# Products of 512 columns issued as two of 256, and their moving operands placed on multiples of 64 bytes

## The chip, the cores and the metric

One core of a Trainium2 chip runs the kernel. The metric is the device time of one execution in microseconds. TensorE multiplies: a product has a stationary operand (`lhsT`, 128 x 128), for which a weight load is recorded ahead of it, and a moving operand (`rhs`), whose columns stream through. VectorE (DVE) and ScalarE (ACT) take results out of PSUM and prepare operands, GpSimd (POOL) does little, and SyncE (SP) issues most of the DMAs.

## The reference

One decoder layer on a sequence of 512 positions with 1024 channels, in float32:

```python
h = rmsnorm(x, ln1_g)
z = h @ w_in                                   # 1024 x 8968
# columns of z: A sliding-window attention, B convolution module, C forgetting attention,
#               D block attention, and 4 x 1024 gate logits
gates = sigmoid(gz + b_gate)
proj  = einsum('bsnc,ncd->bsnd', branches, w_br)   # 4 branches, 512 -> 1024 each
x = x + (gates * proj).sum(branch) @ w_out         # 1024 x 1024
u = causal_depthwise_conv(rmsnorm(x, ln2_g) @ w_up, ffn_conv_w, ffn_conv_b)   # 1024 x 5632, width 3
x = x + (silu(g_ff) * v_ff) @ w_down               # 2816 x 1024
out = rmsnorm(x, final_g)
```

## The kernel before

Float32 products are made of three: every operand is split into a rounded part and a rest (`hi`, `lo`, type float32r), and a product is hi x hi, lo x hi and hi x lo, all added up in one PSUM bank of 512 columns. So nearly all of TensorE's work consists of chains of products `PE.matmul(ps, lhsT=..., rhs=..., start=..., stop=...)`, the first of which (`start`) writes the bank and the others add to it.

The work is a list of *units* (line 254 on). A unit of `t_mm` (line 232, the product on line 243) makes 128 output channels for all 512 positions: a chain of 3 x 8 products (3 x 4 for the branch projections), with the split weights `whi`/`wlo` stationary and the 512 positions of the activations moving. The activations are `hh`/`hl` (the normed input; `hh2`/`hl2`, which the trace also calls hh and hl, for the FFN) or the branch outputs `y`. There are 106 units with hh/hl (62 of the input projection and gates, 44 of the up projection) and 32 with y. `v_units` (line 278, product on line 294) are the other way round: positions stationary, 256 or 264 weight columns moving. `wo_half0` (line 957) and `wo_half1` (line 999) are the two halves of the output projection, with the merged branches stationary and 512 columns of weights moving, the second half's held in `WO` (`woh`, `wol`). `wd_mm` (line 1115) is the down projection: `ah`/`al` stationary, 512 weight columns moving, in the streamed `whi`/`wlo` or in `wdh`/`wdl`, the weights of the last 8 blocks of the second half, which are kept in the tags of `hh` and `hl` (line 1202). In the second half the last 128 positions are worked in two banks of 256 columns each (line 1126), so these products have 256 columns already.

In between the units, *pieces* of the attention heads are put in by a fixed table of steps (`STAGES`, `head_pieces`): scores (lines 451, 452, 565, 566), transposes of the probabilities (479, 596), and the product with the values (`pv`, lines 500 and 619). `pv` of a full head adds to one bank eight products of 512, 384, 256 and 128 columns, two of each, with the same `v` stationary in both of a pair. The order within each engine is the order in which the program writes the instructions (`manual_schedule`); the loop at line 1393 interleaves units, pieces, evictions, weight splits (lines 179, 180) and the steps of the width-31 convolution.

Weights come through a ring of `raw` tiles (2) filled by SP, and are split by ACT (hi) and DVE (lo) into rings `whi` and `wlo` of 3 tiles each.

The pools stand in SBUF like stacks. P0, on the left, holds in this order `ident` (512 bytes of each partition), `hh` and `hl` (16,384 each), `pcA`, `pcB`, `pcC` (368, 496, 512), `nsk`, `sk`, `bfg` (32 each), and then the rings raw, whi and wlo, which are allocated later. Behind it come the pools of the stages: PI, then P1 (attention), then PX (`x1`, `ss2`) and PW (`woh`, `wol`). On the right stands PY, with `acc` and the ring of y tiles (merged branches too), and after it PF (`ah`, `al`).

Of the kernel before, what the change touches and what calls it, by code (L numbers as in the profile page):

```python
# [8 lines left out]
F32 = mybir.dt.float32  # L9
# [9 lines left out]
KD = D // 128  # L19
NT = S // 128  # L20
# [33 lines left out]
def hybrid_layer_kernel(ctx: ExitStack, tc: tile.TileContext, x, ln1_g, w_in, b_gate, b_fgate, sinks,  # L54
# [3 lines left out]
    PE, ACT, DVE, SP = nc.tensor, nc.scalar, nc.vector, nc.sync  # L58
# [16 lines left out]
    P0 = pool("p0")  # L75
    PD = pool("pd", space=PSUM)
    PDR = pool("pdr", space=DRAM)
# [11 lines left out]
    nsk = P0.tile([128, 8], F32, name="nsk")  # L89
    sk = P0.tile([128, 8], F32, name="sk")  # L90
    bfg = P0.tile([128, 8], F32, name="bfg")

    def col_gate(n, j):
        return pcA[:, n * 8 + j:n * 8 + j + 1]
# [129 lines left out]
        return [Half(raw, slice(k, k + 4), slice(0, n)) for k in (0, 4)]  # L224


    class Unit:
        def __init__(self, hs, mm, ev, adv=True):
            self.hs, self.mm, self.ev, self.adv = hs, mm, ev, adv
# [2 lines left out]
    def t_mm(hf, c0, mh, ml, nk):  # L232

        def go(mid=None, at_k=0):
            ps = dense_ps()
            h = hf[0]
            n = 0
            for k in range(nk):
                if mid and k == at_k:
                    mid()  # L240
                wh, wl = h.hi[:, k, c0:c0 + 128], h.lo[:, k, c0:c0 + 128]
                for a, b in ((wh, mh(k)), (wl, mh(k)), (wh, ml(k))):
                    PE.matmul(ps, lhsT=a, rhs=b, start=n == 0, stop=n == 3 * nk - 1)  # L243
                    n += 1
            return ps
        return go
# [16 lines left out]
        return u  # L263


    PY = pool("py", side="right")
    acc = PY.tile([128, KD, S], F32, name="acc")

# [169 lines left out]
    def full_head(br, h):  # L438
        key = (br, h)
        o = live[key] = {}  # L440

        def qk(blocks):
            sk_ = stack[key]
            b2 = sk_["A"] if br == BR_D else sk_["G"]
            nr = 68
            ps = ctxP["s"]()
            c = 0
            for qb in blocks:
                n = (qb + 1) * 128
                qs = slice(qb * 128, qb * 128 + 128)  # L450
                PE.matmul(ps[:, c:c + n], lhsT=sk_["A"][:, qs], rhs=sk_["D"][:, :n], start=True, stop=False)  # L451
                PE.matmul(ps[:, c:c + n], lhsT=b2[:nr, qs], rhs=sk_["E"][:nr, :n], start=False, stop=True)  # L452
                o["s", qb] = ps[:, c:c + n]
                c += n

        def sm(blocks):
            P1 = ctxP["p1"]
            if "P" not in o:
                o["P"] = P1.tile([128, 1280], F32, name="P", tag="P", bufs=2)
                o["nm"] = P1.tile([128, 4], F32, name="nm", tag="nm", bufs=2)  # L460
                o["sm"] = P1.tile([128, 4], F32, name="sm", tag="sm", bufs=2)
                o["rc"] = P1.tile([128, 4], F32, name="rc", tag="rc", bufs=2)
            bias = ctxP["mask"] if br == BR_C else stack[key]["B"]
            for qb in blocks:
                n = (qb + 1) * 128
                soft(o["P"], slice(PO[qb], PO[qb] + n), o["s", qb], n, bias[:, 512 - n:], o["nm"], o["sm"], qb, BIG)

        def norm():
            DVE.reciprocal(o["rc"], o["sm"])
            for qb in range(NT):  # L470
                sl = slice(PO[qb], PO[qb] + (qb + 1) * 128)
                DVE.tensor_scalar(o["P"][:, sl], o["P"][:, sl], o["rc"][:, qb:qb + 1], None, op0=OP.mult)  # L472

        def tr(kbs):
            ps = ctxP["t"]()
            c = 0
            for kb in kbs:
                for qb in range(kb, NT):
                    PE.transpose(ps[:, c:c + 128], o["P"][:, PO[qb] + kb * 128:PO[qb] + kb * 128 + 128], ident)  # L479
                    c += 128  # L480
            o["t", kbs] = ps, c

        TO = {0: 0, 1: 512, 3: 896, 2: 1024}

        def tev(kbs):
            P1 = ctxP["p1"]
            if "PT" not in o:
                o["PT"] = (P1.tile([128, 1280], R32, name="PTh", tag="PTh", bufs=1),
                           P1.tile([128, 1280], R32, name="PTl", tag="PTl", bufs=1))
            ps, c = o["t", kbs]  # L490
            sl = slice(TO[kbs[0]], TO[kbs[0]] + c)
            ACT.activation(o["PT"][0][:, sl], ps[:, :c], AF.Copy)  # L492

        def tlo(kbs):
            ph, pl = o["PT"]
            ps, c = o["t", kbs]
            sl = slice(TO[kbs[0]], TO[kbs[0]] + c)
            DVE.tensor_tensor(pl[:, sl], ps[:, :c], f(ph[:, sl]), op=OP.subtract)

        def pv():  # L500
            ps = ctxP["y"]()
            v = Vt[br, h // 4]
            for kb in range(NT):
                n = (NT - kb) * 128
                for i, pt in enumerate(o["PT"]):
                    PE.matmul(ps[:, kb * 128:], lhsT=v[:, kb, h % 4, :], rhs=pt[:, TO[kb]:TO[kb] + n],  # L506
                              start=kb == 0 and i == 0, stop=kb == NT - 1 and i == 1, skip_group_check=True)
            o["y"] = ps

        def pvev():  # L510
            y_add(br, h, o["y"])

        def pvhl():
            y_out(br, h)
            del live[key]

        return [
            [(lambda: qk((0, 1)), lambda: sm((0, 1)))],
            [(lambda: qk((2,)), lambda: sm((2,)))],
            [(lambda: qk((3,)), lambda: sm((3,)), norm)],  # L520
            [(lambda: tr((0,)), lambda: tev((0,)), lambda: tlo((0,)))],
            [(lambda: tr((1, 3)), lambda: tev((1, 3)), lambda: tlo((1, 3)))],
            [(lambda: tr((2,)), lambda: tev((2,)), lambda: tlo((2,)))],
            [(pv, pvev, pvhl)],
        ]
# [416 lines left out]
    def wo_load():  # L942
        PX = ctxP["px"] = pool("px")
        for t in range(NT):
            xt = PX.tile([128, D], F32, name="x1_%d" % t)
            SP.dma_start(xt, dap(x, t * 128 * D, [[D, 128], [1, D]]))
            x1.append(xt)
        PW = ctxP["pw"] = pool("pw")
        WO["h"] = PW.tile([128, KD, 512], R32, name="woh")
        WO["l"] = PW.tile([128, KD, 512], R32, name="wol")  # L950
        n2["g"] = PW.tile([128, D], F32, name="g2")
        SP.dma_start(n2["g"], dap(ln2_g, 0, [[0, 128], [1, D]]))
        n2["ss"] = PX.tile([128, 2, NT], F32, name="ss2")

    oa = []

    def wo_half0(j0, hs):
        def mm():
            if j0 == 0:
                oa.extend(w_ps() for _ in range(NT))  # L960
            for k in (j0, j0 + 1):
                wh, wl = hs[0].hi[:, k - j0, :], hs[0].lo[:, k - j0, :]
                m = merged[k]
                for t in range(NT):
                    a, b = m[:, 0, t * 128:t * 128 + 128], m[:, 1, t * 128:t * 128 + 128]
                    for i, (l, r) in enumerate(((a, wh), (a, wl), (b, wh))):
                        PE.matmul(oa[t], lhsT=l, rhs=r, start=k == 0 and i == 0, stop=k == KD - 1 and i == 2)  # L967

        def ev(_):
            if j0 == 6:  # L970
                for t in range(NT):
                    wo_ev(t, 0, oa[t])
        add(hs, mm, ev)
# [25 lines left out]
    def wo_half1(t):  # L999
        def mm():  # L1000
            if t == 0:
                n2["hh"] = P0.tile([128, KD, S], R32, name="hh2", tag="hh")
                n2["hl"] = P0.tile([128, KD, S], R32, name="hl2", tag="hl")
            ps = dense_ps()
            for k in range(KD):
                m = merged[k]
                a, b = m[:, 0, t * 128:t * 128 + 128], m[:, 1, t * 128:t * 128 + 128]
                for i, (l, r) in enumerate(((a, WO["h"]), (a, WO["l"]), (b, WO["h"]))):
                    PE.matmul(ps, lhsT=l, rhs=r[:, k, :], start=k == 0 and i == 0, stop=k == KD - 1 and i == 2)  # L1009
            return ps  # L1010

        def ev(ps):
            wo_ev(t, 1, ps)
        u = add([], mm, ev)
        return u
# [99 lines left out]
    def wd_mm(ps, k, t, wh, wl, first_k, last_k):  # L1115
        a, b = ffn["ah"][:, k, t * 128:t * 128 + 128], ffn["al"][:, k, t * 128:t * 128 + 128]
        for i, (l, r) in enumerate(((a, wh), (a, wl), (b, wh))):
            PE.matmul(ps, lhsT=l, rhs=r, start=k == first_k and i == 0, stop=k == last_k and i == 2)  # L1118

    def wd_unit(k0, half, hs):  # L1120
        def mm():
# [84 lines left out]
    for half, end in ((0, NF), (1, KRES)):  # L1206
        for k0 in range(0, end, 4):
            nk = min(4, end - k0)
# [245 lines left out]
    ctxP["pf"].release()  # L1454
    ctxP["px"].release()
    ctxP["w"].release()
    for p in (PDR, PD, P0):
        p.release()


# [40 lines left out]
```

## Time and profile before

| | |
|---|---|
| median of 3 runs | 1014.49 us (1014.19 to 1014.76) |
| profiled execution | 1014.47 us, span 1012.7 us |
| instructions | 12462, of them 4840 products and 4840 weight loads |
| PE busy | 1001.2 us (99%) |
| PEld busy | 824.6 us (81%) |
| DVE busy | 667.0 us (66%) |
| ACT busy | 448.3 us (44%) |
| DMA | 102.18 MB, mean 101 GB/s |

The span runs from the first to the last instruction of the execution. PE's busy time is the union of its products, each from its start to its modelled end; since products overlap, it is no measure of how well the engine is used. The time that a product takes from the next one is the distance between their starts.

### The profile page before, as it was taken

How to read it: one execution, taken by the hardware profiler on the slowest of the kernel's cores; microseconds unless marked ns; L12 is line 12 of the kernel's file. 1: busy time of each engine (PE TensorE's matmuls, PEld its weight loads, DVE VectorE, ACT ScalarE, POOL GpSimd, SP SyncE). 2: the span in 40 equal slices, each digit the busy share in tenths (PEclk: the TensorE clock that was granted, in tenths of full speed). 3: DMA queues.
4: the chain of work that ended last, by engine and by line, in shares of the span. 5: the costliest groups of instructions: out<-in, count | busy, mean ns of one | idle time of the engine just before them, and what ended most of it. 6: DMA issues, size and time to landing. Idle time of an engine off the chain costs nothing.

```text
span 1012.7 us, 12462 instructions
## 1 busy us (share of the span) xinstructions
PE 1001.2 (99%) x4840; PEld 824.6 (81%) x4840; DVE 667.0 (66%) x1188; ACT 448.3 (44%) x782; POOL 23.2 (2%) x49
## 2 busy tenths in 40 slices
PE   8999999999999999999999999999999999999997
PEld 6878887989888888888888888888888888888886
DVE  6557777777878688896665445677776677733404
ACT  6435455455455545556423233443444444432202
POOL 1300000000000000000000000000000000000000
PEclk9999999999999999999999999999999999999999
DMA  7335522132233133232135430232223223334102
GB/s 254 102 113 185 164 85 85 42 105 81 66 108 121 42 83 100 64 99 93 42 125 205 149 125 1 84 125 84 83 94 114 83 84 99 130 124 146 63 1 84
DMA packets 101099, 102.18 MB, mean 101 GB/s; under 512 B 3377, under 2 KB 88544, under 8 KB 101040
## 3 DMA queue, kind: packets, MB, share of 16 engines
q1 hardware_dynamic: 99264, 99.31, 31.0%
q0 software_dynamic: 1200, 1.03, 0.4%
q10 hardware_dynamic: 576, 1.05, 0.3%
q8 instruction: 38, 0.62, 0.2%
q14 instruction: 21, 0.17, 0.1%
HBM read 99.10 MB, written 7.51 MB: 105 GB/s over the span
## 4 chain that ended last, share of the span: by engine, by line
PE 92%; DVE 4%; ACT 2%; issue 1%; DMA 1%; SPq 0%; DVEq 0%; ACTq 0%
PE dps L243 63%; PE wps L1118 8%; PE dps L1118 5%; PE dps L294 4%; PE dps L1009 2%; PE wps L967 2%; PE tps L479 2%; PE yps L506 1%; PE sps L452 1%; PE sps L451 1%; ACT P L434 1%; PE yps L624 1%; DMA raw<-in_w_in_dram 1%; DVE stE L383 1%; DVE P L472 1%
## 5 line engine op out<-in xcount | busy, mean ns | idle before, releaser
L243 PE MATMUL dps<-hh,whi 128*128 128x512 f32 x848 | 336.0, 396 | 0.0
L243 PE MATMUL dps<-hh,wlo 128*128 128x512 f32 x848 | 335.3, 395 | 0.0
L243 PE MATMUL dps<-hl,whi 128*128 128x512 f32 x848 | 335.1, 395 | 0.0
L180 DVE TENSOR_TENSOR wlo<-raw,whi 128x1024 fp32r<-128x1024 f32 (+1 forms) x152 | 185.5, 1222 | 95.4 <-ACT whi L179 95.2
L179 ACT ACTIVATE whi<-raw 128x1024 fp32r<-128x1024 f32 (+1 forms) x152 | 159.6, 1055 | 98.0 <-PE wps L1118 37.9
L243 PEld LDWEIGHTS dps<-hh,wlo 128*128 128x128 f32 x848 | 159.8, 188 | 37.1
L243 PEld LDWEIGHTS dps<-hl,whi 128*128 128x128 f32 x848 | 159.1, 188 | 37.1
L243 PEld LDWEIGHTS dps<-hh,whi 128*128 128x128 f32 x848 | 159.2, 188 | 36.8 <-ACT v L304 0.2
L434 ACT ACTIVATE P<-P,nm 128x128 f32<-128x128 f32 (+2 forms) x96 | 50.9, 531 | 76.4 <-DVE nm L432 75.8
L243 PE MATMUL dps<-y,whi 128*128 128x512 f32 x256 | 83.6, 397 | 0.0
L707 DVE SCALAR_TENSOR_TENSOR co<-hc,pcB,co 128x489 f32<-128x489 f32 (+25 forms) x120 | 82.5, 729 | 0.4
L1082 DVE SCALAR_TENSOR_TENSOR uy<-u,pcC,uy 128x511 f32<-128x511 f32 x88 | 65.8, 747 | 1.5
L243 PEld LDWEIGHTS dps<-y,whi 128*128 128x128 f32 x256 | 48.3, 189 | 10.9
L1074 DVE TENSOR_TENSOR u<-dps,rb 128x512 f32<-128x512 f32 x44 | 30.2, 687 | 37.3 <-PE dps L243 34.6
L243 PE MATMUL dps<-y,wlo 128*128 128x512 f32 x128 | 50.7, 396 | 0.0
L492 ACT ACTIVATE PTh<-tps 128x512 fp32r<-128x512 f32 (+1 forms) x48 | 24.4, 525 | 43.6 <-PE tps L479 43.3
L1118 PE MATMUL wps<-whi,al 128*128 128x512 f32 (+1 forms) x116 | 42.6, 367 | 0.0
L1118 PE MATMUL wps<-whi,ah 128*128 128x512 f32 (+1 forms) x116 | 42.6, 367 | 0.0
L1118 PE MATMUL wps<-wlo,ah 128*128 128x512 f32 (+1 forms) x116 | 42.5, 366 | 0.0
L1096 ACT ACTIVATE ah<-uy 128x512 fp32r<-128x512 f32 x22 | 13.9, 632 | 60.4 <-DVE uy L1095 60.4
L536 ACT ACTIVATE ytmp<-yps 64x512 f32<-64x512 f32 x24 | 14.3, 595 | 48.6 <-PE yps L506 25.0
L1088 ACT ACTIVATE uy<-uy 128x512 f32<-128x512 f32 x22 | 13.9, 632 | 43.7 <-DVE uy L1082 43.7
(250 smaller groups left out, 1291.9 us busy)
## 6 DMA issues: line engine op xcount, KB each, us to landing
raw<-in_w_up_dram SPq DMA_DIRECT2D x22, 1024.0 KB, 5.1
raw<-in_w_in_dram SPq DMA_DIRECT2D x40, 512.0 KB, 3.9
raw<-in_w_in_dram SPq DMA_DIRECT2D x14, 1024.0 KB, 5.1
raw<-in_w_down_dram SPq DMA_DIRECT2D x10, 1024.0 KB, 5.0
raw<-in_w_br_dram SPq DMA_DIRECT2D x16, 512.0 KB, 3.4
Gw<-Gd SPq DMA_DIRECT2D x8, 640.0 KB, 6.9
x<-in_x_dram SPq DMA_DIRECT2D x8, 512.0 KB, 8.4
raw<-in_w_out_dram SPq DMA_DIRECT2D x4, 1024.0 KB, 4.9
```

Source lines behind the costliest of these rows:

```text
L179: yield ACT.activation(self.hi, src, AF.Copy)
L180: yield DVE.tensor_tensor(self.lo, src, f(self.hi), op=OP.subtract)
L243: PE.matmul(ps, lhsT=a, rhs=b, start=n == 0, stop=n == 3 * nk - 1)
L294: PE.matmul(ps[:, :n], lhsT=l, rhs=r[:, k % 4, :], start=not done, stop=len(done) == 3 * KD - 1)
L434: ACT.activation(P[:, sl], P[:, sl], AF.Exp, bias=nm[:, i:i + 1], scale=-1.0, accum_out=sm[:, i:i + 1])
L479: PE.transpose(ps[:, c:c + 128], o["P"][:, PO[qb] + kb * 128:PO[qb] + kb * 128 + 128], ident)
L492: ACT.activation(o["PT"][0][:, sl], ps[:, :c], AF.Copy)
L707: DVE.scalar_tensor_tensor(co[c][:, d:], hc[:, :S - d], col_cw(CW - 1 - d, c), co[c][:, d:], op0=OP.mult, op1=OP.add)
L967: PE.matmul(oa[t], lhsT=l, rhs=r, start=k == 0 and i == 0, stop=k == KD - 1 and i == 2)
L1074: DVE.tensor_tensor(u, ps, n2["rb"], op=OP.mult)
L1082: DVE.scalar_tensor_tensor(y[:, d:], u[:, :S - d], col_fw(2 - d, j), y[:, d:], op0=OP.mult, op1=OP.add)
L1118: PE.matmul(ps, lhsT=l, rhs=r, start=k == first_k and i == 0, stop=k == last_k and i == 2)
```

## The change

A helper `mm2` replaces the call of `PE.matmul` in six places. A product of 512 columns that does not start a bank becomes two products of 256 columns, one after the other, with the same stationary operand and the same bank; a starting product and a narrower one stay as they are. Three empty tiles of 32 bytes in each partition are put in: one in P0 ahead of the rings, one in PX behind `ss2`, and one in a new pool on the right, under PY.

```diff
@@ -89,6 +89,7 @@
     bfg = P0.tile([128, 8], F32, name="bfg")
+    P0.tile([128, 8], F32, name="pad")
@@ -224,6 +225,12 @@
+    def mm2(ps, l, r, start, stop):
+
+        w = r.shape[-1]
+        for c, n in ((0, w),) if start or w < 512 else ((0, 256), (256, 256)):
+            PE.matmul(ps[:, c:c + n], lhsT=l, rhs=r[:, c:c + n], start=start, stop=stop, skip_group_check=True)
+
@@ -240,7 +247,7 @@
                 for a, b in ((wh, mh(k)), (wl, mh(k)), (wh, ml(k))):
-                    PE.matmul(ps, lhsT=a, rhs=b, start=n == 0, stop=n == 3 * nk - 1)
+                    mm2(ps, a, b, n == 0, n == 3 * nk - 1)
@@ -263,6 +270,8 @@
+    PR = pool("pr", side="right")
+    PR.tile([128, 8], F32, name="pad")
     PY = pool("py", side="right")
@@ -503,8 +512,8 @@
                 for i, pt in enumerate(o["PT"]):
-                    PE.matmul(ps[:, kb * 128:], lhsT=v[:, kb, h % 4, :], rhs=pt[:, TO[kb]:TO[kb] + n],
-                              start=kb == 0 and i == 0, stop=kb == NT - 1 and i == 1, skip_group_check=True)
+                    mm2(ps[:, kb * 128:], v[:, kb, h % 4, :], pt[:, TO[kb]:TO[kb] + n], kb == 0 and i == 0,
+                        kb == NT - 1 and i == 1)
@@ -951,6 +960,7 @@
         n2["ss"] = PX.tile([128, 2, NT], F32, name="ss2")
+        PX.tile([128, 8], F32, name="pad")
@@ -964,7 +974,7 @@
-                        PE.matmul(oa[t], lhsT=l, rhs=r, start=k == 0 and i == 0, stop=k == KD - 1 and i == 2)
+                        mm2(oa[t], l, r, k == 0 and i == 0, k == KD - 1 and i == 2)
@@ -1006,7 +1016,7 @@
-                    PE.matmul(ps, lhsT=l, rhs=r[:, k, :], start=k == 0 and i == 0, stop=k == KD - 1 and i == 2)
+                    mm2(ps, l, r[:, k, :], k == 0 and i == 0, k == KD - 1 and i == 2)
@@ -1115,7 +1125,7 @@
-            PE.matmul(ps, lhsT=l, rhs=r, start=k == first_k and i == 0, stop=k == last_k and i == 2)
+            mm2(ps, l, r, k == first_k and i == 0, k == last_k and i == 2)
@@ -1454,7 +1464,7 @@
-    for p in (PDR, PD, P0):
+    for p in (PR, PDR, PD, P0):
```

## Rows read from the trace of the kernel before

**Rows 1.** The page, part 4: shares of the chain that ended last.
```profile
PE 92%; DVE 4%; ACT 2%; issue 1%; DMA 1%; SPq 0%; DVEq 0%; ACTq 0%
```

**Rows 2.** Windows: length, busy us of PE, PEld, DVE, ACT, POOL; PEclk, DMA share, GB/s.
```profile
420.00:440.00 20.00, 20.00 (x106) 16.85 (x105) 19.14 (x52) 7.97 (x18) 0.00 (x0) 1.00 0.31 93
...
960.00:980.00 20.00, 20.00 (x108) 17.06 (x107) 2.45 (x2) 2.13 (x2) 0.00 (x0) 1.00 0.00 1
1001.00:1006.00 5.00, 5.00 (x47) 5.00 (x46) 3.57 (x11) 2.26 (x6) 0.00 (x0) 1.00 0.23 86
```

**Rows 3.** Groups by shape on TensorE: out<-in, shape, count | busy us, mean ns | idle.
```profile
L243 PE MATMUL dps<-hh,whi 128*128 128x512 f32 x848 | 336.0, 396 | 0.0
...
L243 PE MATMUL dps<-y,whi 128*128 128x512 f32 x256 | 83.6, 397 | 0.0
L243 PE MATMUL dps<-y,wlo 128*128 128x512 f32 x128 | 50.7, 396 | 0.0
L1118 PE MATMUL wps<-whi,al 128*128 128x512 f32 x88 | 34.7, 395 | 0.0
...
L967 PE MATMUL wps<-whi,mg 128*128 128x512 f32 x64 | 20.1, 393 | 0.0
L1118 PE MATMUL dps<-whi,al 128*128 128x512 f32 x42 | 16.7, 397 | 0.0
...
L294 PE MATMUL dps<-whi,hh 128*128 128x256 f32 x96 | 13.7, 284 | 0.0
...
L967 PE MATMUL wps<-wlo,mg 128*128 128x512 f32 x32 | 12.5, 391 | 0.0
L1118 PE MATMUL dps<-wdh,ah 128*128 128x512 f32 x24 | 9.5, 394 | 0.0
```

**Rows 4.** The chain in order of time (start us, length us, what): products of 512 columns.
```profile
588.57 22.12 PE wps L967 x96
...
617.15 5.60 PE dps L1009 x24
...
645.84 237.63 PE dps L243 x1020
...
883.47 61.30 PE wps L1118 x264
...
984.09 16.80 PE dps L1118 x72
```

**Rows 5.** The same chain: pieces whose products have 256 columns.
```profile
175.81 5.70 PE dps L294 x48
...
966.53 0.71 PE wps L1118 x6
...
1000.89 5.47 PE wps L1118 x48
```

**Rows 6.** Timeline of TensorE, 1002:1013 (start, length, line): first and last of 39.
```profile
1001.76 0.28 PE L1118 MATMUL wps<-wdh,ah 128*128 128x256 f32 x1
...
1006.07 0.28 PE L1118 MATMUL wps<-wdh,al 128*128 128x256 f32 x1
```

**Rows 7.** Groups of weight loads, with the same columns.
```profile
L243 PEld LDWEIGHTS dps<-hh,whi 128*128 128x128 f32 x848 | 159.2, 188 | 36.8 <-ACT v L304 0.2
...
L506 PEld LDWEIGHTS yps<-PTl,v 128*128 128x128 f32 x64 | 12.0, 188 | 1.4
```

**Rows 8.** The chain: four transposes; two stretches off TensorE, first and last piece of each.
```profile
263.94 0.44 PE tps L479 x4
...
291.45 0.56 DVE P L432
...
299.34 0.33 PE tps L479
...
429.57 0.60 ACT ytmp L536
...
451.93 0.63 PE tps L753 x4
```

## The prediction

> **What bounds the kernel now.** I read first the chain that ended last, then the chain in order of time to get the price of one product, then the timeline of the last stretch, then the groups by shape for the counts, and last the windows for what the other engines do. The chain lies on TensorE for 92% of the span [rows 1], and the granted clock is 1.00 in every window [rows 2], which is 2.4 GHz. The reader should not take the 396 ns mean of a product of 512 columns [rows 3] for its price: products overlap, and what counts is the distance from start to start. 1020 products in 237.63 us are 233.0 ns each; the 72 of line 1118 near the end are 233.3 [rows 4]. 512 columns at 2.4 GHz would be 213.3 ns, so about 20 ns of each product are something else.
>
> What that is can be seen at the products of 256 columns that the kernel already has. Those with whi or wlo as moving operand cost 5.70 us / 48 = 118.8 ns (line 294) and 0.71 / 6 = 118.3 ns (line 1118, 14 such pieces) [rows 5]. Two of them are 236.6 to 237.5 ns: worse than one of 512. But the 48 of the last part of the down projection, whose moving operands are wdh and wdl, run from 1001.76 to 1006.07 us in 38 steps, 113.4 ns each [rows 5, 6]. Two of those are 226.8 ns.
>
> Why the two differ decides the case. It is not the traffic: the dear ones of line 1118 run while VectorE is busy 2.45 us of 20 and the DMA share is 0.00, the cheap ones while VectorE is busy 3.57 us of 5 and the DMA share is 0.23 [rows 2]. The stationary operand (ah, al) is the same. What differs is where the moving operand lies. In P0 the tiles ahead of the rings add up, each rounded up to 32 bytes, to 34,784 bytes, that is 543.5 times 64: raw, whi and wlo begin 32 bytes past a multiple of 64. wdh and wdl carry the tags of hh and hl, which stand on a multiple (512 and 16,896 bytes into the pool). That reading is counted from the tile sizes; the trace shows only the two prices.
>
> **The change part by part.** *The split.* A starting product stays whole, so the 106 + 32 units of line 243 keep 138 of their 3 x 848 + 256 + 128 = 2928 products, and 2790 are split [rows 3]. Line 967: 64 + 32 less 4 = 92; line 1009, the same shape of loop: 92. Line 1118: 3 x 88 less 4 = 260 into wps, 3 x (42 + 24) less 3 = 195 into dps [rows 3]. Line 506: one of the two products of kb = 0 in each of 16 heads, 16. Together 3445, so PE carries 3445 more products and as many more weight loads.
>
> Price of a pair: 2 x 113.4 = 226.8 ns. For 2438 of line 243 and 72 of line 1118 that is no guess about the place: their moving operand lies in the very slots (hh, hl) in which wdh and wdl were timed. Saved:
> line 243: 2790 x (233.0 - 226.8) = 17.3 us;
> line 967: 22.12 us / 96 = 230.4 ns [rows 4], so 92 x 3.6 = 0.3 us;
> line 1009: 5.60 / 24 = 233.3 ns, so 92 x 6.5 = 0.6 us;
> line 1118: 61.30 / 264 = 232.2 ns, so 260 x 5.4 = 1.4 us, and 195 x 6.5 = 1.3 us;
> line 506: 0.1 us. Sum 21.0 us.
>
> *The weights.* The second half has the same stationary operand. Does it pay a load, or none? The pairs of line 506 share their weights too, and the trace holds a load of 188 ns for each of the 64 second products [rows 7]; they are not skipped. A load lies under the product before it as long as that is long enough: transposes of 128 columns, each with a load, follow each other at 0.44 us / 4 = 110 ns [rows 8], so the load needs at most 110 and a half gives it 113.4. The cover is 3 ns thin. If loads took as long as halves of 118.4 allow, the pair would cost 236.8; bounds for a half: 110 to 118.8. I take 113.4, since that row has a new load under each half; less would need loads shorter than any there, and is left out of the range.
>
> *The place.* The pad in P0 moves raw, whi, wlo and all that is opened behind them by 32 bytes; the one in PX brings woh and wol back to a multiple of 64; the one on the right moves acc and the y ring. The 288 products of 256 columns in line 294 [rows 3] should fall from 118.8 to 113.4: 1.6 us. The 84 of line 1118: 84 x 4.9 = 0.4 us. The attention products of 256 columns (lines 506, 565, 566, 624; 128 of them) lie between 0 and 128 x 5.4 = 0.7 us; 0.3 taken, since many sit next to shorter products. The 96 of 264 columns: rows of 1056 bytes, every other one off by 32 before and after, 0. ah and al, behind the right pad, move off the multiple as stationary operands: whi stands so in line 243 today, and its load takes 188 ns [rows 7], no more than the others; 0 taken, and at most what the bounds of a half hold. Sum so far 23.3 us.
>
> *What TensorE then waits for.* A few stretches of the chain lie on other engines, four of 8 to 14 us in the attention steps, from a head's scores to the transposes (one of them 291.45 to 299.34 us), and one where VectorE is busy 19.14 us of 20 (429.57 to 451.93) [rows 2, 8]. There a faster TensorE only arrives earlier and waits. With the 8% of the chain off PE [rows 1], less some 20 us at the start and the end where nothing is split, about 60 us give nothing: 60 / 0.233 x 6.2 ns = 1.6 us; 1.5 taken, 0 to 7.0 as bounds (below).
>
> Net 23.3 - 1.5 = 21.8 us. The profiled execution took 1014.47 us (span 1012.7 and 1.8 around it), the median of the runs 1014.49: **992.7 us**.
>
> Against splitting speaks the Trainium skill, "TensorE: Matmul & The Clock Gate", section "Back-to-back issue gap": a warm product costs its columns at 2.4 GHz and a fixed 2.5 ns. By that 512 columns are 215.8 ns, two halves 218.3, and 3445 splits an estimated 8.6 us more, some 1023 us. The trace does not agree on the size: it has 233.0 for 512 and 113.4 for 256 columns [rows 4, 6], so the surplus more than halves with the width.
>
> **The rivals.** *A: a fixed price for each product, whatever the place.* Then halves cost what they cost in lines 294 and 1118, 118.8. For it: two lines of very different stages agree on 118.3 to 118.8, and only one stretch of 48 shows less. Against it: that stretch is steady, and busier than the dear one. A half decides at 233.0 / 2 = 116.5 ns. Price: 2790 x 4.6 + 92 x 7.2 + 92 x 4.3 + 260 x 5.4 + 195 x 4.3 = 16.1 us more, 1030.6 us. That is the rule of the Trainium skill just named (section "Back-to-back issue gap") in rows of this kernel.
>
> *B: VectorE becomes the bound of the attention stages.* If all between 160 and 460 us gives nothing, 23.3 x 300 / 1000 = 7.0 us are lost instead of 1.5: 998.2 us. For it: 19.14 of 20 us busy [rows 2]. Against: that is the worst window, and the chain is on PE for most of the stage.
>
> *C: the pads do not reach the rings* (another rounding than I count). Then only the 2510 pairs in the slots of hh and hl gain, 2510 x 6.2 = 15.6 us, the other 935 cost 237.2 instead of about 233, 3.9 us more, and nothing comes from the place: 15.6 - 3.9 - 1.5 = 10.2 us, 1004.3 us. Against it: the sizes count out at just half a multiple.
>
> **How the numbers follow.** Forecast 0.71, A 0.08, B 0.13, C 0.06, something between forecast and no change 0.02. The forecast's own range is 988 (a half of 113.0, all of the small terms, no wait) to 997. Upward it reaches to B and to a half of 114.7 ns in the busy stages (1.3 x 2 x 3445 = 9.0 us): the range is 987 to 1002, with 0.15 left out above it and 0.03 below. A measurement of this kernel tells 0.2%, 2 us: faster 0.90 (forecast, B, C), the same 0.02, slower 0.08 (A).
>
> **What would show it.** In the chain, a unit of line 243 (one whole product and 23 pairs) takes 233 + 23 x 226.8 = 5.45 us instead of 5.60, and its products start 113 apart; line 294 takes 48 x 113.4 = 5.44 us instead of 5.70; PEld counts 3445 more loads; the two stretches of [rows 8] keep their length. The forecast is wrong if halves on hh start over 116 ns apart; the place is wrong if those on whi stay at 118 while those on hh do not; B shows as idle time of PE in front of transposes, above all between 160 and 460 us.

## The result, and the profile after

The changed kernel takes 1026.46 us (median of 4 runs, 1026.38 to 1026.82) against 1014.53 us before on the same chip (1014.19 to 1014.76): a ratio of 1.0118, with a 95% interval of 1.0106 to 1.013. It is slower by 12 us where 21.8 us less were forecast.

The page of the kernel after, its parts 1 and 4:

```profile
span 1025.0 us, 19365 instructions
...
PE 1013.3 (99%) x8285; PEld 994.2 (97%) x8285; DVE 667.2 (65%) x1188; ACT 448.5 (44%) x782; POOL 23.2 (2%) x49
...
PE 91%; DVE 5%; ACT 2%; issue 1%; DMA 1%; SPq 0%; DVEq 0%; ACTq 0%
```

The chain is on TensorE as it was [rows 1], and the span grew by 12.3 us. The chain in order of time (start us, length us, what), the pieces that answer to [rows 4, 5]; line 232 is the new helper, in which the products of lines 243, 967, 1009 and 1118 now are, and line 303 is the old 294:

```profile
177.59 5.72 PE dps L303 x48
...
592.97 22.58 PE wps L232 x188
...
651.23 242.52 PE dps L232 x1998
893.75 62.57 PE wps L232 x524
...
958.44 0.70 PE wps L232 x6
...
996.01 17.04 PE dps L232 x144
1013.04 5.69 PE wps L232 x48
```

The reader should put each beside its piece of before. The 1020 products of the up projection, now 1998 instructions, take 242.52 instead of 237.63 us; line 967's 22.58 instead of 22.12; line 1118's 62.57 instead of 61.30 and 17.04 instead of 16.80. Line 303, which only the pads touch, takes 5.72 where it took 5.70. And the very stretch from which the forecast had its price, the last 48, went from 5.47 to 5.69 us: 118.5 ns a product, not 113.4.

The groups by shape and the loads (columns as in [rows 3, 7]):

```profile
L232 PE MATMUL dps<-hh,wlo 128*128 128x256 f32 x1696 | 339.0, 281 | 0.0
...
L232 PEld LDWEIGHTS dps<-hh,wlo 128*128 128x128 f32 x1696 | 268.6, 189 | 5.3
```

Each half has a load, and the load is as long as before, 189 ns in the mean where it was 188 [rows 7].

Windows in the attention stages, in the down projection and in the last stretch (columns as in [rows 2]):

```profile
420.00:440.00 20.00, 20.00 (x171) 19.79 (x169) 19.56 (x50) 10.42 (x27) 0.00 (x0) 1.00 0.32 93
960.00:980.00 20.00, 20.00 (x171) 20.00 (x170) 6.91 (x9) 5.73 (x8) 0.00 (x0) 1.00 0.09 28
1013.00:1019.00 6.00, 5.72 (x49) 5.52 (x47) 3.88 (x12) 2.26 (x6) 0.00 (x0) 1.00 0.23 87
```

The clock is at 1.00, 2.4 GHz, as before, and TensorE is busy throughout the first two. So it isn't a wait: the products themselves follow each other more slowly. From start to start in the timeline, summed over each group: the products of hh and hl went from 594.9 to 605.3 us (+10.4), those of y from 90.1 to 89.5 (-0.6), line 1118's with whi and wlo from 100.6 to 102.3 (+1.6), lines 967 and 1009 from 44.7 to 45.6 (+0.9), the products of wdh and wdl +0.5, line 294's +0.1. That is 12.9 us of the 12.3; small changes elsewhere take back 0.6.

### The profile page after: what moved, and what is told of

It reads as the page before. It is cut to its first block, busy times and chain, and to the rows that moved or that the text cites. A ratio compares the mean times of both kernels' runs of the same rounds, so it can differ in the third digit from the quotient of the medians.

```text
span 1025.0 us, 19365 instructions
## 1 busy us (share of the span) xinstructions
PE 1013.3 (99%) x8285; PEld 994.2 (97%) x8285; DVE 667.2 (65%) x1188; ACT 448.5 (44%) x782; POOL 23.2 (2%) x49
## 4 chain that ended last, share of the span: by engine, by line
PE 91%; DVE 5%; ACT 2%; issue 1%; DMA 1%; SPq 0%; DVEq 0%; ACTq 0%
PE dps L232 69%; PE wps L232 10%; PE dps L303 4%; PE tps L488 2%; PE yps L232 1%; PE sps L461 1%; PE sps L460 1%; ACT P L443 1%; DVE wlo L181 1%; DMA raw<-in_w_in_dram 1%; DVE P L441 1%; DVE stE L392 1%; PE yps L633 1%; DVE P L481 1%; ACT stD L391 0%
## 5 line engine op out<-in xcount | busy, mean ns | idle before, releaser
L232 PE MATMUL dps<-hh,whi 128*128 128x256 f32 (+1 forms) x1590 | 341.6, 291 | 0.0
L232 PE MATMUL dps<-hh,wlo 128*128 128x256 f32 x1696 | 339.0, 281 | 0.0
L232 PE MATMUL dps<-hl,whi 128*128 128x256 f32 x1696 | 338.5, 281 | 0.0
L232 PEld LDWEIGHTS dps<-hh,wlo 128*128 128x128 f32 x1696 | 268.6, 189 | 5.3
L232 PEld LDWEIGHTS dps<-hl,whi 128*128 128x128 f32 x1696 | 260.9, 189 | 0.0
L232 PEld LDWEIGHTS dps<-hh,whi 128*128 128x128 f32 x1590 | 248.2, 189 | 0.8 <-ACT v L313 0.2
L232 PE MATMUL dps<-y,whi 128*128 128x256 f32 (+1 forms) x480 | 83.2, 287 | 0.0
L232 PE MATMUL dps<-y,wlo 128*128 128x256 f32 x256 | 50.4, 278 | 0.0
L232 PE MATMUL wps<-whi,ah 128*128 128x256 f32 (+1 forms) x200 | 43.0, 284 | 0.0
L232 PE MATMUL wps<-wlo,ah 128*128 128x256 f32 x204 | 43.0, 281 | 0.0
```

What stands on the lines that cost most here:

```text
L232: PE.matmul(ps[:, c:c + n], lhsT=l, rhs=r[:, c:c + n], start=start, stop=stop, skip_group_check=True)
```

## The experiments

Below, the *distance* is the number of bytes, in a partition, from the start of the moving operand to the stationary operands of the same stretch, modulo 256; in whole kernels it is counted from the tile sizes, and the traces show only the prices. Three kernels undo or shift parts of the change, two place everything anew, and four are chains of products alone.

**Bare chains at every distance.** Moving operands and weights from two tiles, each chain 24 products of 512 or 48 of 256 columns; the weights' tile is entered at 16 places 32 bytes apart, the moving operand's at two.

```
for m0 in (0, 8):
    for d in range(16):
        chain("s%d_%d" % (4 * m0, 32 * d), 256, m0, 8 * d, 48, False)
    ...
        chain("w%d_%d" % (4 * m0, 32 * d), 512, m0, 8 * d, 24, False)
    ...
        chain("p%d_%d" % (4 * m0, 32 * d), 256, m0, 8 * d, 48, True)
```

> This kernel leaves the whole layer out: it runs chains of products with nothing beside them, and its time is no time of the layer. A moving tile of 8 rows of 2048 bytes and a stationary tile of 8 blocks of 512 bytes; per chain the stationary tile starts d = 0, 32, ..., 480 bytes past a fixed place. Chains named s are 48 products of 256 columns, each with its own row; w are 24 of 512 columns; p are 24 pairs of halves with the same weights; once with the moving operand on a multiple of 128 bytes (s0, w0, p0) and once 32 bytes past it (s32, w32, p32). Theory 1 (distance): the load of the next weights and the stream of the moving operand disturb each other by where both lie, not by whether the moving operand stands on a multiple of 64; half price 113.4 ns (5.44 us a chain) where they lie 64 bytes apart modulo 128, 118.5 (5.69 us) elsewhere; chains w 5.44 us at 64, 5.60 elsewhere. Rival (fixed price): all s and p chains cost the same whatever d, 5.44 us if the traffic of the layer makes the 118.5, 5.69 us if the product itself does. The old reading (place of the moving operand alone): all of s0 5.44, all of s32 5.69 us.

Measured: 580.27 us in all. The chain of waits; s are halves with new weights each, w are whole products, p pairs of halves with the same weights, 16 distances in each piece, once for each place of the moving operand:

```profile
28.21 90.94 PE s L85 x768
119.14 89.15 PE w L85 x384
208.29 90.94 PE p L85 x768
299.23 90.87 PE s L85 x768
390.10 89.11 PE w L85 x384
```

The second half of the list repeats the first, though all moving operands lie 32 bytes further: the absolute place does nothing. The mean of a half is 118.4 ns, of a whole product 232.2, and p costs what s costs. Within a piece the price goes by the distance (ns from start to start, worked out from the timeline, the first products of each chain left out):

```
distance    0      32     64     96     128    160    192    224
512 cols    226.7  233.2 to 234.3 at 32 to 160 and 224   228.9 (192)
256 cols    120.0  118.3  117.8  117.3  118.8  120.0  117.8  117.8
```

At 256 bytes and beyond the same prices come again. Two halves cost 234.6 to 240.0, more than a whole product at nearly every distance, and most where the whole product is cheapest. One chain differs: at 224, the first behind the pairs, a half took 116.7. No chain here shows 113.4, which theory 1 expected at 64.

**The pads alone.** The new kernel with its helper looping over `((0, w),)`, so nothing is split.

> The three pads without the split. Theory 1 (distance): of the products of 512 columns only those on y come to lie 64 apart from their weights, 384 x up to 6 ns = up to 2.3 us less: 1012 to 1015 us. Rival (fixed price): nothing in it depends on the place, 1014.5 us. The old reading: the 256-column products of line 294 fall to 113.4, 1.6 to 2 us less: 1012.5 us.

```
-        for c, n in ((0, w),) if start or w < 512 else ((0, 256), (256, 256)):
+        for c, n in ((0, w),):
```

Measured: 1012.65 us, ratio 0.9979 (0.997 to 0.9989). Two pieces of its chain of waits:

```profile
644.05 236.77 PE dps L232 x1020
...
998.52 5.69 PE wps L232 x48
```

The pads are worth 2 us, but not where I put them, on line 294 (5.70 and 5.72 us a chain), nor where theory 1 had them, on y (90.1 us in both kernels); that both came near the time is luck. The whole products of the up projection fall from 233.0 to 232.1 ns, and those with hl, which come to distance 0 for a part of the ring, to 227. The last 48 rise from 5.47 to 5.69 us although nothing of them is changed but the place of ah and al, 32 bytes lower. So the place of the *stationary* operand counts too: wdh and wdl have not moved at all.

**The split alone.** The three pads left out of the new kernel.

> The split without the pads: hh and whi lie 96 bytes apart modulo 128, y and whi 0, wdh and ah 64. Theory 1 (distance): hh pairs at about 118.5 a half as in the changed kernel, y pairs at 118.5 instead of 115.5 (+2 us), the last 144 + 48 products of the down projection 113.4 instead of 118.3 (-0.9 us): 1026 to 1029 us. Rival (fixed price): the same as the changed kernel, 1026.5 us, with the last stretch at 118 as well. The old reading: hh pairs at 113.4 (they have not moved): below 1005 us.

```
-    P0.tile([128, 8], F32, name="pad")
-    PR = pool("pr", side="right")
-    PR.tile([128, 8], F32, name="pad")
-        PX.tile([128, 8], F32, name="pad")
```

Measured: 1023.89 us, ratio 1.0088 (1.0072 to 1.0105). Its chain:

```profile
651.79 239.97 PE dps L231 x1998
...
1010.42 5.45 PE wps L231 x48
```

Here hh and hl lie on the very bytes on which the forecast timed a half at 113.4, and halves on them cost 118.0. With ah and al back in place, the last 48 are at 113.5 again. The time is 2 us under theory 1's range, since halves on hh took 118.0 and not 118.5. The two parts together cost 4.8 us more than the sum of each (-2.1 and +9.2 us, against +11.9 for both): the pads, good for whole products, are bad for the halves on hh and hl (118.7 with them, 118.0 without) and on wdh and wdl (118.3 and 113.4), though good for those on y (115.5 and 118.8).

**The split at distances 64 and 192.** Two small tiles are moved ahead of hh, so hh and hl go up by 64 bytes, with pads of other sizes in PX and PF.

> The split, with hh and hl moved by 64 bytes (two small tiles stand ahead of them instead of behind), so that hh-whi, y-whi, whi-mg, woh-mg and wdh-ah all lie 64 bytes apart modulo 128; whi-ah lie 0 apart. Everything is still on multiples of 64. Theory 1 (distance): the 2438 pairs on hh fall from 2 x 118.7 to 2 x 113.5 to 115.5 ns: 15 to 25 us less than the changed kernel, 1001 to 1011 us, faster than before. Rival (fixed price): 1026.5 us, as the changed kernel.

```
+    nsk = P0.tile([128, 8], F32, name="nsk")
+    sk = P0.tile([128, 8], F32, name="sk")
     (both ahead of hh, and gone from behind it)
-        PX.tile([128, 8], F32, name="pad")
+        PX.tile([128, 24], F32, name="pad")
+        PF.tile([128, 8], F32, name="pad")
```

Measured: 1005.49 us, ratio 0.991 (0.9895 to 0.9925). Its chain:

```profile
606.68 5.45 PE dps L232 x47
...
641.19 233.07 PE dps L232 x1998
874.27 62.34 PE wps L232 x524
...
993.20 5.66 PE wps L232 x48
```

The same number of products and loads as after, with the same split, is 21 us faster. Halves on hh and hl are at 114 ns, most steps 113 or 114; those of whi and wlo with ah and al, at 0 or 128 here, are not (118.1), and the last 48, now at 192, lost their cheap price, against what theory 1 expected of them. That a product has a fixed price whatever the place is refuted by this run, and the forecast's price for a half exists, at another distance.

**A map.** Bare chains again: five regions of the memory, weights above and below the moving operand, weights in steps of 512 and 2048 bytes, the two parts of the weights at equal and at different distances.

> Like the first chains this leaves the layer out and times bare products: one tile of 176 KB a partition, moving rows 2048 bytes apart, weights in blocks 512 or 2048 bytes apart; names begin with w for 24 products of 512 columns and s for 24 pairs of halves, and end with the distance from the moving operand to the weights modulo 256: zero, sixtyfour, half (128), threeq (192). up a to e: weights 32, 64, 96, 128, 156 KB above the moving operand; down f, g: 156 and 92 KB below it; hl: the layer's order hi, lo, hi with two distances; wide and tail: weights 2048 bytes apart, tail at the distance of the cheap last stretch of the kernel before. From the first chains: 512 columns cost 226.7 ns at distance zero, 228.9 at threeq, 233.4 at sixtyfour and half; halves never fell under 117.3, so what makes 113.4 is not the distance modulo 256 alone. Theory 1a (the region counts too): halves cost 113.4 in some of up b to e or down f, g and in tail, 117 to 120 in up a; w chains 226.7 at zero in every region. Rival (the step of the weights counts): only wide and tail show 113.4, all of up and down 117 to 120. Rival (fixed price, and the place of the stretch before was chance): all s chains 117 to 120, tail too.

Measured: 631.69 us in all. From its chain of waits (w whole, s halves; the region's letter, then the distance: threeq is 192; hl: the distances of hi and lo):

```profile
26.99 5.44 PE wupazero L82 x24
32.43 5.60 PE wupasixtyfour L82 x24
...
115.51 5.45 PE wupezero L82 x24
120.96 5.60 PE wupesixtyfour L82 x24
...
159.78 5.45 PE wdowngzero L82 x24
...
456.83 5.75 PE sdowngzero L82 x48
...
491.06 5.69 PE shlzerohalf L82 x48
...
508.06 5.65 PE shlsixtyfoursixtyfour L82 x48
...
519.30 5.50 PE shlsixtyfourthreeq L82 x48
524.80 5.65 PE shlhalfzero L82 x48
...
615.78 5.67 PE stail L82 x48
```

Region, direction and step make no difference: distance 0 is 5.44 or 5.45 us for 24 products of 512 columns everywhere, 226.7 to 227.1 ns, and 64 is 233.3. (At 128 the map has 232.2 in every region, where the first chains had 233.4.) The chain tail, at the distance of the cheap last stretch, takes 5.67 us and not 5.44. Halves whose two weights lie at 64 and 192 cost 114.6, near the 114.4 that the split kernel of the last experiment has on hh; with 0 and 128, as in the changed kernel, they cost 118.6 or 117.6, where that kernel has 118.7.

**Everything at distance 0, whole.** hi and lo share a tile, so that both parts keep one place; pads bring hh, hl, the ring, y, woh, ah and al to the same place modulo 256. Against the kernel with the pads alone:

> No split. Every moving operand and every weight of the dense products put at one and the same place modulo 256 bytes: hi and lo of a split share one tile of the ring (lo 4352 bytes behind hi), and the pads in P0, on the right, in PX and PF bring the ring, y, woh and ah to where hh and hl stand. Theory 2 (what counts is the distance from moving operand to weights modulo 256; 512 columns cost 226.7 ns at distance zero and 229 to 234 elsewhere, halves 120.0 at zero): 2928 x 6.4 + 96 x 3.7 + 96 x 6.6 + 462 x 5.9 = 22.4 us less, 420 products of 256 columns at 120 instead of 118 to 119 0.8 us more, 1.5 us lost in waits: 994 us, 992 to 998. Rival (a price of the instruction, the chains being special because nothing runs beside them): 1012 to 1015 us, a unit still 5.6 us.

```
-                self.hi = P0.tile(shape, R32, name="whi", tag="whi", bufs=NSP)
-                self.lo = P0.tile(shape, R32, name="wlo", tag="wlo", bufs=NSP)
+                n = shape[1] * shape[2]
+                w = P0.tile([128, 2112], R32, name="whl", tag="whl", bufs=NSP)
+                l0 = 1056 if n > 1024 else 1088
+                self.hi = w[:, :n].rearrange("p (k c) -> p k c", k=shape[1])
+                self.lo = w[:, l0:l0 + n].rearrange("p (k c) -> p k c", k=shape[1])
...
-    PR.tile([128, 8], F32, name="pad")
+    PR.tile([128, 24], F32, name="pad")
-        PX.tile([128, 8], F32, name="pad")
+        PX.tile([128, 24], F32, name="pad")
+        PF.tile([128, 56], F32, name="pad")
```

Measured: 999.01 us (997.46 to 999.37), ratio 0.9842 (0.9827 to 0.9857): faster than both kernels, with the products of before. The profiled execution, 997.46 us, in its chain:

```profile
637.33 231.22 PE dps L235 x1020
868.54 59.84 PE wps L235 x264
...
967.27 16.35 PE dps L235 x72
983.62 5.76 PE wps L235 x48
```

231.22 / 1020 = 226.7 ns, the price of the bare chain to the tenth. The groups' sums fall by 18.6 us and the span by 17.0: some 1.5 us came back as longer waits of TensorE, in front of transposes above all. The median is 5 us above what was expected and 1 us out of the range: 22.4 us were counted for the products.

**The same places, split.**

> The same places, and the split of the change on top. Theory 2: halves at distance zero cost 120.0 ns, the dearest of all, so the split, which gains nothing anywhere at this place, costs 3445 x (240.0 - 226.7) = 46 us over the unsplit kernel: about 1040 us (1036 to 1042), 14 us more than the changed kernel, although every moving operand stands on a multiple of 64. Old reading (a moving operand on a multiple of 64 makes a half cheap): 992 us. Fixed price: 1026 us.

```
-        for c, n in ((0, w),):
+        for c, n in ((0, w),) if start or w < 512 else ((0, 256), (256, 256)):
```

Measured: 1037.73 us, ratio 1.0228 (1.0211 to 1.0245). Its chain, the piece of the up projection:

```profile
658.53 244.52 PE dps L235 x1998
```

13.30 us more for 978 splits, 13.6 ns each; halves at 120.0 ns. The whole costs 38.7 us over the unsplit kernel, where 46 were expected. So in the best place for whole products the split does the most harm of the places tried.

**The last stretch by itself.** Bare halves in the order of the down projection's last part, and with one operand held, one and two at a time, at eight distances.

> Bare products again (the layer is left out), 256 columns, 48 a chain: the order of the last stretch of the down projection (one down: hi moving with weights a, lo with a, hi with b), the order of line 243 (up), one moving row and one weight throughout a triple (plain), and one without a second weight tile (oneb) or moving tile (onem); one: the same half of a row throughout, pair: both halves; at all distances modulo 256 in steps of 32. What it asks: at distance 64 the chain called tail cost 117.8 ns a half and the last stretch of the kernel before 113.4. If the order of the operands makes the difference, onedownsixtyfour costs 113.4 (5.44 us) and oneplainsixtyfour 117.8 (5.65 us). If it is the state in which a chain begins, all chains at 64 cost 117.8, and the 113.4 stays open. At zero all cost 120.

Measured: 408.43 us. From its chain (a is distance 32):

```profile
34.25 5.75 PE onedownzero L102 x48
...
80.32 5.67 PE onedowna L102 x48
...
125.75 5.65 PE onedownsixtyfour L102 x48
...
154.02 5.65 PE pairdownsixtyfour L82 x48
```

Neither the order nor the number of tiles matters: distance 64 is 117.8 in each form, where the kernel before has 113.4 to 114.

**What ran before the chain.** The same halves, each chain behind another lead of 24 products, once with VectorE and once with transfers beside it.

> Bare products with the layer left out, as in the earlier chains: 48 products of 256 columns at one distance (64, 224, 192 or 96 bytes modulo 256 from the moving operand to the next weights), each chain behind a different lead of 24 products: 512 columns at the same distance, 512 at distance 0, 512 at distance 128, 128 columns, 264 columns; once in two chains of 24 as in the last part of the down projection; once with VectorE busy beside it; once with four output transfers beside it. Theory (the price is settled by the distance alone): 117.8 ns at 64, 224 and 192 and 117.3 at 96 behind every lead, as in the earlier bare chains; then the 113.4 ns of the last stretch of the kernel before stays unexplained. Rival (at some distances two rhythms are possible, and what ran before a stretch chooses one): at distance 64 at least one lead gives 113 to 114 ns, most likely that of 512 columns at the same distance, which is what precedes the stretch in the kernel, and the others 117.8. Second rival (other engines' accesses to the memory choose): the difference shows with VectorE or the transfers beside the chain. Whole run by the theory about 470 us, by either rival not over 10 us less.

```
run("leadhalf" + dn, rows(128, 8), 512)
run("afterhalf" + dn, rows(d, 16), 256)
```

Measured: 394.83 us in all (some 470 had been counted). From its chain, at distance 64 and 192:

```profile
49.28 5.66 PE aftersamesixtyfour L99 x48
...
60.40 5.66 PE afterzerosixtyfour L99 x48
66.06 5.58 PE leadhalfsixtyfour L99 x24
71.64 5.45 PE afterhalfsixtyfour L99 x48
77.09 2.63 PE leadnarrowsixtyfour L99 x24
79.72 5.50 PE afternarrowsixtyfour L99 x48
...
99.19 2.73 PE tailonesixtyfour L99 x24
...
110.23 5.45 PE aftervecsixtyfour L99 x48
...
238.61 5.44 PE afterhalfthreeq L99 x48
...
277.58 5.65 PE aftervecthreeq L99 x48
```

Here the 113.4 appears: at 64 and at 192 one chain of 48 halves takes 5.66 or 5.44 us, on the same bytes. The chain behind products of 512 columns at distance 128 has the lower price; at 64 it stayed through the chains that followed (114.6 in the mean behind the products of 128 columns, 113.5 in the two short chains of the tail's order), at 192 it was lost behind the next lead. Beside VectorE's work and beside the transfers the price stayed what it had been, 113.5 at 64 and 117.8 at 192. At 96 and 224 no chain was under 116.6, but there too the price is not one: 117.4 to 119.7 at 96, 116.7 to 118.9 at 224. The rival is borne out, though not with the lead that it named.

## Why the prediction was wrong

**The step that failed** is "Why the two differ decides the case ... What differs is where the moving operand lies", and with it the price of a pair, 2 x 113.4 = 226.8 ns: on hh and hl a pair took 237.4. The two prices were read rightly, and place does matter, but the pattern of multiples of 64 was found for the moving operand alone. I had one stretch of 48 products and took from it a rule that fitted whi and hh by half a multiple; the distance to the stationary operand fitted the same rows, and I held that operand to be the same on both sides ("The stationary operand (ah, al) is the same"), so it had no place in the reading. Two runs show it against me: with the split alone the moving operand stays on the bytes of the cheap stretch and a half costs 118.0; with the pads alone the cheap stretch loses its price while its moving operand stays.

**"2438 of line 243 ... is no guess about the place."** It was the same place of hh, with other weights: whi and wlo are 0 or 128 from hh after the change, at which bare halves cost 120.0 and 118.8; in the kernel they were 118.3 to 119.1, that is 237 a pair against 233.0 for a whole product. It was the sign that the prediction named for itself: halves on hh start over 116 ns apart. y's halves, at 115.5, are the only ones of line 243 that gained (-0.6 us).

**"ah and al ... move off the multiple as stationary operands: 0 taken."** The wrong argument: the load's duration, 188 to 189 ns, does not show what its place costs the products beside it. The last 48 paid 0.22 us, and only the bounds of a half held it; the 144 halves on wdh and wdl before them took 17.04 us, where the split alone has 16.34.

**The place, 1.6 us for line 294 and 0.4 for line 1118's 84**: nothing. 5.70 became 5.72; the pieces of six stayed at 0.70 to 0.71. The prediction had said what this would mean: the place is wrong if those on whi stay at 118, though it expected those on hh to fall meanwhile, and they did not.

**The weights and the waits** decided nothing. The weights came out as forecast: 3445 more products and loads, a load under each half. Of the two stretches of [rows 8] off TensorE the first kept its 7.9 us; in the second the chain is off TensorE for 36.1 us (419.46 to 455.56) instead of 22.4, which the prediction did not expect. It cost nothing: the transposes ahead of it start 3.7 us later than before and those behind it 3.6. That a load needs at most 110 ns was right: 24 products of 128 columns, each with a load, take 2.63 us in the last bare run at each of its four distances, 109.6 each, so the load by itself does not hold the half at 118. That the gain would be lost to VectorE (rival B) was not tried by the change itself, since there was no gain; the whole version at distance 0 lost only some 1.5 us of 18.6 so.

**Rival A** came nearest, 1030.6 us with halves at 118.8, and had 0.08. Its outcome is right and its reason wrong: the price is not the same whatever the place, since the same split at other distances is faster than before (0.991). With the pads and without them hh lies where halves are dear, 118.7 and 118.0. Its chance was too low all the same: 288 halves on line 294 and 84 on line 1118 [rows 3, 5] stood against one stretch of 48, and the doubt should have been as large as the sample was small. **Rival C**, pads that do not reach the rings, is out: with the pads alone the products on hh and hl changed their price.

The Trainium skill, "TensorE: Matmul & The Clock Gate", section "Back-to-back issue gap", has a fixed 2.5 ns beside the columns at 2.4 GHz, in its formula for the gap of a single product. Where everything lies at distance 0 the traces agree with the form: 226.7 and 120.0 are 213.3 and 106.7 ns and 13.3 more each; not with the size, and at 64 and 192 not with the form, where the price goes to 113.4 or 117.8 for 256 columns. By its 2.5 ns the split would have cost an estimated 8.6 us, 2.5 a split; the two kernels at distance 0 differ by 13.6 ns a split, near the 13.3.

**What stays open.** Why 256 bytes, no run tells. Whether it is the product's own weights or those of the next product that count has no simple answer in the traces. Neither decides alone: with the pads alone, where hi lies at 0 from hh and hl and lo at 128, the step behind hi x hl (own and next weights at 0) is 227 ns, behind hi x hh (own 0, next 128) 232 and behind lo x hh (own 128, next 0) 234. Nor do the two together: in the map with hi at 64 and lo at 0, the step whose own and next weights are both at 64 is 226, while in the chain with all at 64 the steps alternate between 231 and 236. What makes one chain at 64 or 192 run at 113.4 and another at 117.8 is shown only to depend on what ran before it.

## What to carry to other kernels

Before splitting or padding for TensorE, take the distance between the two operands, not the place of one: here whole products of 512 columns with hi, lo and moving operand at one place modulo 256 bytes gave 1.6% of the whole time, with no product more. A price that one short stretch shows is a hypothesis; a run that changes one operand's place at a time settles it. A split is only worth it where a half costs less than half, here under 116.5 ns, and the same split gave ratios from 0.991 to 1.0228 by nothing but pads of 32 to 224 bytes, the order of small tiles, and hi and lo in one tile.

## What the hardware showed unexpectedly

The price of a product of 512 columns in this data type went from 226.7 to 234.3 ns and of 256 columns from 113.4 to 120.0, at a granted clock of 1.00 in the windows read, by the distance of its operands modulo 256 bytes; absolute place, region and step of the weights made no difference. The order of the two is nearly opposite: distance 0 is the best for 512 columns and the worst for 256. And at distances 64 and 192 a stream of halves has two rhythms, 113.4 and 117.8, and at 64 the lower one lasted across other products of 128, 264 and 512 columns.
